# The third weight sum of a seven-product unit: added by a DMA instead of GpSimd, and its product one place later

## The chip, the core and the metric

One core of a Trainium2 chip runs the whole program. The metric is the device time of one execution in microseconds (us); runs of one kernel are compared by their median. The engines are TensorE (PE, matrix products; PEld are its weight loads), VectorE (DVE), ScalarE (ACT), GpSimd (POOL) and SyncE (SP, which here only issues DMAs). Each engine works through its own instruction list in order, and an instruction that waits holds back everything behind it on that engine. DMAs are issued by SP, ACT or POOL and run on sixteen DMA engines.

## What is computed

One step of a two-branch encoder layer over 576 frames (512 of a prompt, 64 of a stream), in float32: a gated feed-forward block, a mixer (a state-space branch, band attention and a matrix memory, merged by gates), and a second feed-forward block.

```python
def swiglu(x, w_in, w_out):
    a, b = jnp.split(x @ w_in, 2, axis=-1)
    return (jax.nn.silu(a) * b) @ w_out

def layer(x, lp, st):
    h = x + 0.5 * swiglu(rmsnorm(x, lp['norm_ffn1']), lp['w_ffn1_in'], lp['w_ffn1_out'])
    mix, new_st = mixer(rmsnorm(h, lp['norm_mix']), lp, st)
    h = h + mix
    h = h + 0.5 * swiglu(rmsnorm(h, lp['norm_ffn2']), lp['w_ffn2_in'], lp['w_ffn2_out'])
    return h, new_st
```

Nearly all the time goes into the products with the weights: `w_ffn1_in` and `w_ffn2_in` (1024 x 8192), their `w_out` (4096 x 1024), and the mixer's `w_in` (1024 x 9752).

## The kernel before

**Units of seven products.** Most of the weight products are done in the manner of Strassen and Winograd: a block of 1024 rows of weights by two column tiles of 128 is taken as four quarters (0 to 3, each 128 partitions x 512), the activations as two halves of the frames (288 each), and eight quarter products become seven. Such a unit needs four sums of weight quarters: X1 = q0 + q1, X2 = q1 + q2, X3 = X1 + q2, X4 = X3 + q3; the products A11, A22 and A21 use quarters 0, 2 and 3 as they are. There are 115 units: 40 in each feed-forward layer (28 that make gated hidden tiles, `swiglu`, and 12 that add to the residual) and 35 in the mixer.

**Splitting.** Each weight operand is split into a high and a low part: ScalarE copies it to a reduced format (tile ph, line 288), VectorE subtracts that from the original (tile pl, line 289). Each product is then 12 matmuls of 128 x 288 on PE (line 616): four row tiles by three combinations of high and low parts.

**Where the sums come from.** `fetch_sums` has SP load quarters 0 and 1 side by side into a tile x12 (ring "wx", four buffers, 128 x 1024), and returns a function that adds quarters 1 and 2 onto it by an adding DMA that GpSimd issues (line 461): x12 then holds X1 and X2. `fetch` has SP load quarters 0, 2 and 3 (ring "wr", five buffers; line 467). `operand` makes X3 and X4 by GpSimd additions (line 472). In the feed-forward layers both are made in place, over X1 and then over X3, so X3's sum waits until X1 has been split, and X4's until X3 has. In the mixer they go to two buffers of the ring "wy", both made when the first of them is asked for.

**Order.** `stream` walks through the units' products in a fixed order (the tuples `order` in `pairs` for the mixer and in `ffn`; a 1 ahead of a product means that it belongs to the unit before). For each product it makes the operand of the product five places on (`AHEAD`), then issues the matmuls, then the read-out of the accumulator. ph and pl have six buffers each, so a split can be six operands ahead of PE. `make` starts the loads of a unit two units ahead, and the adding DMA of the unit after next when X3 is made. From this text a scheduler puts each engine's instructions into their final order, by its own estimate of when each can run.

**Accumulators.** A product adds onto an accumulator that an earlier one began: X3, A22 and X2 onto that of X1, A21 onto that of X4. Between two such products the running sum is read out (by ScalarE: uv, line 533, g, line 627, P, line 632; by VectorE: lines 542, 629, 635, 639, 655), and PE must wait for that read-out. The mixer has three banks for this, the feed-forward layers six. Between the products the mixer's PE also works on the branches' own small matmuls (`tick`, `jobs`).

Of the kernel before, what the change touches and what calls it, by code (L numbers as in the profile page):

```python
# [28 lines left out]
ALU = mybir.AluOpType  # L29
# [52 lines left out]
class Hybrid:  # L82
# [369 lines left out]
    def fetch_sums(self, desc):  # L452


        nc = self.nc
        i = len(self.splan)
        self.splan.append(desc)
        src = self.I["sblk"][i].rearrange("p (q c) -> p q c", q=4)
        x12 = self.ring("wx", shape=(128, 2, 512))
        nc.sync.dma_start(x12, src[:, 0:2, :])  # L460
        return {"x12": x12, "src": src}, lambda: nc.gpsimd.dma_start(x12, src[:, 1:3, :], accum_op=ALU.add)  # L461
# [6 lines left out]

    def operand(self, raw, t):

        x12 = raw["x12"]
        add = lambda o, one, two: self.nc.gpsimd.tensor_tensor(o, one, two, op=ALU.add)  # L472
        if not self.mixer:

            if t in (self.T_X3, self.T_X4):
                add(x12[:, 0, :], x12[:, 0, :], raw[2 if t == self.T_X3 else 3])
            x3 = x4 = x12[:, 0, :]
        else:
            if t in (self.T_X3, self.T_X4) and "x3" not in raw:
                raw["x3"], raw["x4"] = self.ring("wy"), self.ring("wy")  # L480
                add(raw["x3"], x12[:, 0, :], raw[2])
                add(raw["x4"], raw["x3"], raw[3])
            x3, x4 = raw.get("x3"), raw.get("x4")
        return self.parts({self.T_X1: x12[:, 0, :], self.T_X2: x12[:, 1, :], self.T_X3: x3, self.T_X4: x4,
                           self.T_A11: raw[0], self.T_A22: raw[2], self.T_A21: raw[3]}[t])

    def stream(self, seq, order, banks):

# [31 lines left out]
    def pairs(self, seq):  # L520

        nc = self.nc
        order = ((0, self.T_X1), (0, self.T_A11), (1, self.T_A22), (0, self.T_X4), (0, self.T_X3), (1, self.T_X2),
                 (0, self.T_A21))
        H = (slice(0, FH), slice(FH, T))

        def tmp(ps, scale):  # L530
            o = self.gp.tile([128, FH], F32, name="uv", tag="uv", bufs=4)
            with self.tc.high_priority(offset=EVAC):
                nc.scalar.activation(o, ps, AF.Copy, scale=scale)  # L533
            return o

        def emit(ps, scale, other=None, op=None):
            def go(dst, a=0, b=FH, func=None):
                with self.tc.high_priority(offset=EVAC):
                    if other is None:
                        nc.scalar.activation(dst, ps[:, a:b], func or AF.Copy, scale=scale)  # L540
                        return
                    nc.vector.scalar_tensor_tensor(dst, ps[:, a:b], scale, other[:, a:b], op0=ALU.mult, op1=op)
                if func:
                    nc.scalar.activation(dst, dst, func)
            return go

        def pair(tiles, done):
            ((name, c1), s1, put1), ((_, c2), s2, put2) = tiles
            o = {}

            def on(t, ps):
                if t == self.T_X1:
                    o["v"] = tmp(ps, s1)
                elif t == self.T_X4:
                    o["m6"] = tmp(ps, s2)
                elif t == self.T_A11:
                    put1(1, H[1], emit(ps, s1, o["v"], ALU.add))
                elif t == self.T_X3:
                    o["u"] = tmp(ps, s2)
                elif t == self.T_A21:  # L560
                    put2(1, H[1], emit(ps, s2, o["u"], ALU.subtract))
                elif t == self.T_A22:
                    put2(0, H[0], emit(ps, -s2, o["m6"], ALU.add))
                else:
                    put1(0, H[0], emit(ps, s1))
                    if done:
                        done()
            return (name, 0, c1, c2), self.T, on

        self.stream([pair(*p) for p in seq], order, lambda n: {self.T_X1: n % 2, self.T_X4: 2, self.T_A11: 2})  # L570
# [113 lines left out]
    def ffn(self, x, g0, win, wout, name, last=(0, 1)):  # L684
# [3 lines left out]
        nc = self.nc  # L688
# [63 lines left out]
        def unit(c, j):  # L752
            def done(g):
                got[c, j] = g
                flush()
            return (win, 0, 4096 + at(c, j), at(c, j)), self.T, self.swiglu(done)

        def out(c, m):
            def done():
                free[0] = True  # L760
                if c == 2:
                    self.hidden_tiles(name)
                flush()
            return (wout, 1024 * c, 256 * m, 256 * m + 128), self.T2, self.residual(x, m, done if m == 3 else None)
# [4 lines left out]
        seq = [unit(0, j) for j in range(NPLAIN, 8)]  # L769
        for c in range(1, 4):  # L770
            seq += [unit(c, j) for j in range(2)] + [out(c - 1, m) for m in range(4)] + [unit(c, j) for j in range(2, 8)]
        order = ((0, self.T_X1), (1, self.T_A22), (0, self.T_A11), (1, self.T_A21), (0, self.T_X3), (1, self.T_X2),
                 (0, self.T_X4))
        self.stream(seq, order, lambda n: {self.T_X1: n % 3, self.T_A11: 3, self.T_X4: 4 + n % 2})
        self.drain()
# [833 lines left out]
```

## Time and profile before

| | |
|---|---|
| median of 3 runs | 1939.52 us (1937.3 to 1940.52) |
| the profiled execution | 1944.79 us, its span 1943.1 us |
| mean clock that TensorE was granted | 0.991 of full speed |
| first feed-forward layer / mixer's units / second feed-forward layer | about 50 to 600 / 610 to 1205 / 1410 to 1940 us |
| data moved by DMA | 294.69 MB, 152 GB/s on the mean |

The profile is of one execution. Its page gives, for each engine, busy time, share of the span and instruction count; the costliest groups of instructions by line, with the tile written and the tiles read (`wx<-wx,wr`), their count, their busy time, the mean of one in ns, and after the second bar the time in which the engine sat idle just before them and what ended most of it. A list of waits says who waited for whom: total us, how many times, the longest. A table of stretches gives the busy us of each engine in a part of the span, with instruction counts in brackets. The timeline lists instructions with start and duration in us (`x2`: two in a row). Among the DMA rows, an issue has its count, its size and the median us from issue to landing, and q0 is the queue of the DMAs that GpSimd issues (packets, MB, share of the sixteen engines' time).

### The profile page before, as it was taken

The page shows a single profiled execution, that of the slowest core. Times are in us where ns is not written, and L with a number is a line of the kernel's source. Part 1 is how long each engine was busy: PE and PEld are TensorE (multiplying, and loading weights), DVE is VectorE, ACT ScalarE, POOL GpSimd, SP SyncE. Part 2 cuts the span into 40 slices and gives each one's busy share as a digit, 9 for nine tenths or more (in the row PEclk, how much of TensorE's full clock was granted, in tenths as well). Part 3 has the DMA queues.
Part 4 walks back from the last instruction along what each step waited for, and adds up shares of the span by engine and source line. Part 5 has one row for each costly group of instructions (what it writes and reads, how often), then busy time and mean ns, then how long its engine had stood idle before and what let it go on. Part 6 is the DMA issues. An engine that isn't in the chain of part 4 may idle for free. (4 is left out here: it accounts for less than half of the span.)

```text
span 1943.1 us, 37678 instructions
## 1 busy us (share of the span) xinstructions
PE 1887.2 (97%) x13901; PEld 1823.6 (94%) x13901; DVE 1524.6 (78%) x2715; ACT 1089.5 (56%) x2486; POOL 680.1 (35%) x656
## 2 busy tenths in 40 slices
PE   9999999999999999999999998999999999999998
PEld 8899999999999878888888888999999999999998
DVE  8998998988768767667777775745898888988865
ACT  4554654655544777767675765324555455554544
POOL 5343333333202234323435353440233334334311
PEclk9999999999999999899999999999999999999999
DMA  7267666666742545753667557742236666666631
GB/s 241 74 160 173 159 163 163 159 172 163 185 131 80 156 117 159 200 147 108 183 165 183 155 152 213 241 143 88 77 99 165 163 157 172 166 157 167 159 94 60
DMA packets 129440, 294.69 MB, mean 152 GB/s; under 512 B 14289, under 2 KB 26193, under 8 KB 129257
## 3 DMA queue, kind: packets, MB, share of 16 engines
q1 hardware_dynamic: 100072, 205.67, 32.7%
q0 software_dynamic: 19696, 72.10, 20.5%
q10 hardware_dynamic: 9488, 14.53, 2.6%
q8 instruction: 109, 1.79, 0.4%
q14 instruction: 75, 0.61, 0.1%
HBM read 272.87 MB, written 19.38 MB: 150 GB/s over the span
## 5 line engine op out<-in xcount | busy, mean ns | idle before, releaser
L616 PE MATMUL acc<-TH,ph 128*128 128x288 f32 x3220 | 968.0, 301 | 27.4 <-ACT uv L533 11.8
L616 PE MATMUL acc<-TL,ph 128*128 128x288 f32 x3220 | 955.4, 297 | 0.6 <-DVE TL L289 0.6
L616 PE MATMUL acc<-TH,pl 128*128 128x288 f32 x3220 | 955.0, 298 | 1.0 <-DVE pl L289 0.9
L616 PEld LDWEIGHTS acc<-TH,ph 128*128 128x128 f32 x3220 | 607.5, 189 | 46.9 <-ACT uv L533 15.5
L616 PEld LDWEIGHTS acc<-TL,ph 128*128 128x128 f32 x3220 | 609.4, 189 | 4.9 <-issue 3.7
L616 PEld LDWEIGHTS acc<-TH,pl 128*128 128x128 f32 x3220 | 608.4, 189 | 4.8 <-DVE pl L289 2.2
L289 DVE TENSOR_TENSOR pl<-wr,ph 128x512 fp32r<-128x512 f32 x471 | 429.4, 919 | 76.9 <-ACT ph L288 64.5
L288 ACT CAST ph<-wr 128x512 fp32r<-128x512 f32 x471 | 287.9, 620 | 267.9 <-PE acc L616 141.3
L289 DVE TENSOR_TENSOR pl<-wx,ph 128x512 fp32r<-128x512 f32 x390 | 328.1, 845 | 44.5 <-ACT ph L288 37.9
L288 ACT CAST ph<-wx 128x512 fp32r<-128x512 f32 x390 | 237.4, 621 | 201.3 <-POOL wx L472 110.2
L472 POOL TENSOR_TENSOR wx<-wx,wr 128x512 f32<-128x512 f32 x160 | 246.3, 1539 | 188.2 <-DVE pl L289 150.4
L461 POOL DMA_DIRECT2D wx<-in_sblk x115 | 101.6, 901 | 524.1 <-DMA wx<-in_sblk 154.7
L260 PE MATMUL acc<-YH,ph 128*128 128x256 f32 (+1 forms) x768 | 226.5, 298 | 6.3 <-ACT YH L288 5.8
L260 PE MATMUL acc<-YL,ph 128*128 128x320 f32 (+1 forms) x768 | 227.1, 297 | 2.3 <-DVE YL L339 1.9
L260 PE MATMUL acc<-YH,pl 128*128 128x256 f32 (+1 forms) x768 | 226.5, 296 | 0.1
L260 PEld LDWEIGHTS acc<-YH,ph 128*128 128x128 f32 x768 | 145.4, 190 | 6.9 <-ACT YH L288 5.9
L260 PEld LDWEIGHTS acc<-YL,ph 128*128 128x128 f32 x768 | 145.4, 189 | 3.5 <-DVE YL L339 3.3
L260 PEld LDWEIGHTS acc<-YH,pl 128*128 128x128 f32 x768 | 145.2, 189 | 0.3 <-DVE pl L289 0.3
L472 POOL TENSOR_TENSOR wy<-wx,wr 128x512 f32<-128x512 f32 x35 | 56.2, 1605 | 136.0 <-DVE pl L289 120.0
L655 DVE SCALAR_TENSOR_TENSOR R<-acc,R 128x288 f32<-128x288 f32 x168 | 75.7, 450 | 18.6 <-PE acc L616 18.1
L288 ACT CAST TH<-g 128x288 fp32r<-128x288 f32 x120 | 51.6, 434 | 59.8 <-POOL g L641 34.6
L289 DVE TENSOR_TENSOR pl<-wy,ph 128x512 fp32r<-128x512 f32 x70 | 59.8, 857 | 29.6 <-ACT ph L288 26.6
(320 smaller groups left out, 2393.4 us busy)
## 6 DMA issues: line engine op xcount, KB each, us to landing
wr<-in_sblk SPq DMA_DIRECT2D x345, 256.0 KB, 3.6
wx<-in_sblk SPq DMA_DIRECT2D x115, 512.0 KB, 3.8
wx<-in_sblk POOLq DMA_DIRECT2D x115, 512.0 KB, 6.8
wr<-in_wblk SPq DMA_DIRECT2D x126, 256.0 KB, 3.0
R<-scr_rows ACTq DMA_DIRECT2D x12, 576.0 KB, 5.9
gs<-g SPq DMA_DIRECT2D x20, 288.0 KB, 4.5
g<-gs POOLq DMA_DIRECT2D x20, 288.0 KB, 3.9
y<-ys POOLq DMA_DIRECT2D x12, 288.0 KB, 3.8
```

Source lines behind the costliest of these rows:

```text
L260: nc.tensor.matmul(ps[:, :n], wt[:, wsl], xx[:, k0 + k, a:a + n], start=(k == 0 and i == 0), stop=(k == nk - 1 and i == 2))
L288: self.nc.scalar.copy(hi, src)
L289: self.nc.vector.tensor_tensor(lo, src, hi.bitcast(F32), op=ALU.subtract)
L461: return {"x12": x12, "src": src}, lambda: nc.gpsimd.dma_start(x12, src[:, 1:3, :], accum_op=ALU.add)
L472: add = lambda o, one, two: self.nc.gpsimd.tensor_tensor(o, one, two, op=ALU.add)
L616: self.nc.tensor.matmul(ps, wt[:, wsl], xx[:, kk, :], start=(start and kk == 0 and i == 0), stop=(kk == 3 and i == 2), skip_group_check=True)
L655: self.nc.vector.scalar_tensor_tensor(o, ps, scale, o, op0=ALU.mult, op1=ALU.add)
```

## The change

The third sum is no longer made by GpSimd. As soon as X1 has been split, an adding DMA that GpSimd issues adds quarter 2 from HBM onto the X1 half of x12, in place, in the feed-forward layers and in the mixer alike. GpSimd adds only X4: in place in the feed-forward layers, into one buffer of "wy" in the mixer. In both orders X3 moves back one place: behind the earlier unit's X2 in the feed-forward layers, ahead of X4 (which had been first) in the mixer.

```diff
     def operand(self, raw, t):
 
-        x12 = raw["x12"]
-        add = lambda o, one, two: self.nc.gpsimd.tensor_tensor(o, one, two, op=ALU.add)
-        if not self.mixer:
-
-            if t in (self.T_X3, self.T_X4):
-                add(x12[:, 0, :], x12[:, 0, :], raw[2 if t == self.T_X3 else 3])
-            x3 = x4 = x12[:, 0, :]
-        else:
-            if t in (self.T_X3, self.T_X4) and "x3" not in raw:
-                raw["x3"], raw["x4"] = self.ring("wy"), self.ring("wy")
-                add(raw["x3"], x12[:, 0, :], raw[2])
-                add(raw["x4"], raw["x3"], raw[3])
-            x3, x4 = raw.get("x3"), raw.get("x4")
-        return self.parts({self.T_X1: x12[:, 0, :], self.T_X2: x12[:, 1, :], self.T_X3: x3, self.T_X4: x4,
-                           self.T_A11: raw[0], self.T_A22: raw[2], self.T_A21: raw[3]}[t])
+        nc, x12 = self.nc, raw["x12"]
+        x4 = x13 = x12[:, 0, :]
+        if t == self.T_X4:
+            if self.mixer:
+                x4 = self.ring("wy")
+            nc.gpsimd.tensor_tensor(x4, x13, raw[3], op=ALU.add)
+        parts = self.parts({self.T_X1: x13, self.T_X2: x12[:, 1, :], self.T_X3: x13, self.T_X4: x4,
+                            self.T_A11: raw[0], self.T_A22: raw[2], self.T_A21: raw[3]}[t])
+        if t == self.T_X1:
+            nc.gpsimd.dma_start(x13, raw["src"][:, 2, :], accum_op=ALU.add)
+        return parts
...
-        order = ((0, self.T_X1), (0, self.T_A11), (1, self.T_A22), (0, self.T_X4), (0, self.T_X3), (1, self.T_X2),
+        order = ((0, self.T_X1), (0, self.T_A11), (1, self.T_A22), (0, self.T_X3), (0, self.T_X4), (1, self.T_X2),
                  (0, self.T_A21))
...
-        order = ((0, self.T_X1), (1, self.T_A22), (0, self.T_A11), (1, self.T_A21), (0, self.T_X3), (1, self.T_X2),
+        order = ((0, self.T_X1), (1, self.T_A22), (0, self.T_A11), (1, self.T_A21), (1, self.T_X2), (0, self.T_X3),
                  (0, self.T_X4))
```

In the changed file the lines behind `operand` are three lower: the adding DMA of the first sums is on line 462, GpSimd's add on 477, the new adding DMA on 481, the matmuls on 613.

How the built programs differ, first on GpSimd, in the residual units of the first feed-forward layer. The names with numbers are single tiles: wx_3441 (before) and wx_3443 (after) belong to unit 20, wx_3590 to unit 21, wx_3725 to unit 22, wx_3858 to 23, wx_3991 to 24. Before:

```order
L461 DMA wx_3725<-in_sblk 128x1024
L472 TENSOR_TENSOR wx_3441<-wx_3441,wr_3586 128x512
L472 TENSOR_TENSOR wx_3441<-wx_3441,wr_3588 128x512
L461 DMA wx_3858<-in_sblk 128x1024
L472 TENSOR_TENSOR wx_3590<-wx_3590,wr_3721 128x512
L472 TENSOR_TENSOR wx_3590<-wx_3590,wr_3723 128x512
L461 DMA wx_3991<-in_sblk 128x1024
```

After:

```order
L462 DMA wx_3725<-in_sblk 128x1024
L481 DMA wx_3443<-in_sblk 128x512
L477 TENSOR_TENSOR wx_3443<-wx_3443,wr_3588 128x512
L462 DMA wx_3858<-in_sblk 128x1024
L481 DMA wx_3590<-in_sblk 128x512
L477 TENSOR_TENSOR wx_3590<-wx_3590,wr_3723 128x512
L462 DMA wx_3991<-in_sblk 128x1024
```

The new DMA (128 x 512) stands where the add of X3 stood: behind the DMA of the first two sums of the unit after next, and ahead of the add of X4.

Second, ScalarE at the same place, the copies to high parts from A11 of unit 20 to A22 of unit 20. Before they are A11, A21 (unit 19), X3, X2 (unit 19), X4, X1 of unit 21, A22:

```order
L288 CAST ph_3762<-wr_3584 128x512
L288 CAST ph_3779<-wr_3439 128x512
L288 CAST ph_3798<-wx_3441 128x512
L288 CAST ph_3816<-wx_3292 128x512
L288 CAST ph_3835<-wx_3441 128x512
L288 CAST ph_3860<-wx_3590 128x512
L288 CAST ph_3878<-wr_3586 128x512
```

After:

```order
L288 CAST ph_3763<-wr_3584 128x512
L288 CAST ph_3780<-wr_3441 128x512
L288 CAST ph_3797<-wx_3292 128x512
L288 CAST ph_3816<-wx_3443 128x512
L288 CAST ph_3835<-wx_3443 128x512
L288 CAST ph_3860<-wx_3590 128x512
L288 CAST ph_3879<-wr_3586 128x512
```

X2 of unit 19 (tile wx_3292) now stands ahead of X3 of unit 20; X3, X4 and the next unit's X1 follow each other without another operand between.

Third, ScalarE in the mixer, from A22 of unit 61 to A21 of unit 62; uv and P are read-outs of accumulators, the g row is a branch's own work. Before, the two rows that read wy are X4 and X3, the one that reads wx is X2 of unit 61:

```order
L288 CAST ph_12819<-wr_12345 128x512
L540 ACTIVATE P_12559<-acc_12510 128x288
L1152 ACTIVATE g_12860<-P_12559,cst_143 128x579
L288 CAST ph_12841<-wy_12838 128x512
L288 CAST ph_12866<-wy_12837 128x512
L288 CAST ph_12883<-wx_12169 128x512
L533 ACTIVATE uv_12817<-acc_12804 128x288
L533 ACTIVATE uv_12835<-acc_12725 128x288
L533 ACTIVATE uv_12900<-acc_12887 128x288
L288 CAST ph_12902<-wr_12566 128x512
```

After, X3 comes first, from x12 itself (wx_12331), then X4 (wy_12841) and X2 (wx_12150):

```order
L288 CAST ph_12797<-wr_12325 128x512
L530 ACTIVATE uv_12795<-acc_12703 128x288
L537 ACTIVATE P_12538<-acc_12489 128x288
L1149 ACTIVATE g_12836<-P_12538,cst_143 128x579
L530 ACTIVATE uv_12814<-acc_12801 128x288
L288 CAST ph_12817<-wx_12331 128x512
L530 ACTIVATE uv_12877<-acc_12864 128x288
L288 CAST ph_12843<-wy_12841 128x512
L288 CAST ph_12860<-wx_12150 128x512
L288 CAST ph_12879<-wr_12545 128x512
```

One of the three read-outs uv now stands right behind the copy of X3, two ahead of it.

## What was predicted

> **What bounds the kernel now.** I read the page's first part, then the table of stretches, then what TensorE waited for.
>
> ```profile
> PE 1887.2 (97%) x13901; PEld 1823.6 (94%) x13901; DVE 1524.6 (78%) x2715; ACT 1089.5 (56%) x2486; POOL 680.1 (35%) x656
> ```
>
> TensorE (PE) is busy 97% of the span, so everything that a faster helper could return lies in the other 3%, 56 us. Stretches, with busy us of each engine and matmuls in brackets (of 50 to 100, 300 to 350, and the mixer):
>
> ```profile
> core 0: us, PE busy (x) PEld busy (x) DVE busy (x) ACT busy (x) POOL busy (x), PEclk, DMA share, GB/s
> 50.00:100.00 50.00, 46.85 (x325) 45.08 (x325) 48.16 (x88) 28.87 (x64) 17.93 (x12) 0.97 0.27 75
> 300.00:350.00 50.00, 50.00 (x377) 50.00 (x376) 44.48 (x68) 25.77 (x53) 18.18 (x16) 1.00 0.65 165
> 633.00:1205.00 572.00, 546.34 (x3957) 494.36 (x3956) 403.66 (x855) 402.15 (x1098) 220.17 (x224) 0.99 0.60 160
> ```
>
> In the middle of a feed-forward layer PE never stops: 377 matmuls in 50 us are 0.1326 us each, so a product (12) takes 1.59 us and a unit of seven products 11.14 us. That is the **pace** everything else has to keep. The mixer holds most of the idle time (26 us), and the first units (50 to 100) another 3. What PE waited for, longest first:
>
> ```profile
> PE acc L616 <- ACT uv L533: 11.8, 12, 2.9
> PE acc L616 <- DVE g L542: 4.6, 4, 1.6
> PE acc L616 <- ACT g L627: 2.6, 7, 0.6
> PE acc L616 <- DVE P L635: 2.0, 8, 0.3
> PE acc L616 <- DVE pl L289: 0.9, 3, 0.4
> ```
>
> Almost all are accumulators that ScalarE or VectorE had not read out yet; an operand (pl) was late three times. So the third sums do not hold PE now.
>
> **What goes and what comes.** GpSimd's groups and its DMA issues (count, then busy us and mean ns; the last two rows give min/median/max ns):
>
> ```profile
> L472 POOL TENSOR_TENSOR wx<-wx,wr 128x512 f32<-128x512 f32 x160 | 246.3, 1539 | 188.2 <-DVE pl L289 150.4
> L461 POOL DMA_DIRECT2D wx<-in_sblk x115 | 101.6, 901 | 524.1 <-DMA wx<-in_sblk 154.7
> L472 POOL TENSOR_TENSOR wy<-wx,wr x35: 1260/1294/3738, 600.2 to 1171.8; 128x512 f32<-128x512 f32 x35
> L472 POOL TENSOR_TENSOR wy<-wy,wr x35: 1276/1297/1817, 602.6 to 1174.3; 128x512 f32<-128x512 f32 x35
> ```
>
> 80 feed-forward adds of 1.54 us and 35 mixer adds of 1.29 us go: 123 + 45 = 168 us of GpSimd. 115 more issues of 0.90 us come: 104 us. GpSimd is busy 35%, so the 64 us themselves are worth nothing on PE. Two side effects matter more. One unit of the feed-forward layer, row by row in the timeline (start, us, engine):
>
> ```profile
> 335.22 0.88 POOL L461 DMA_DIRECT2D wx<-in_sblk  x1 [5.70 <-DVE TL L289]
> 339.65 0.67 DVE L289 TENSOR_TENSOR pl<-wx,ph 128x512 fp32r<-128x512 f32 x1
> 340.40 1.45 POOL L472 TENSOR_TENSOR wx<-wx,wr 128x512 f32<-128x512 f32 x1 [2.21 <-DVE pl L289]
> 340.75 2.49 DVE L289 TENSOR_TENSOR pl<-wx,ph 128x512 fp32r<-128x512 f32 x2
> 341.88 0.62 ACT L288 CAST ph<-wx 128x512 fp32r<-128x512 f32 x1 [0.87 <-POOL wx L472]
> 342.70 0.62 ACT L288 CAST ph<-wx 128x512 fp32r<-128x512 f32 x1
> 343.52 0.68 DVE L289 TENSOR_TENSOR pl<-wx,ph 128x512 fp32r<-128x512 f32 x1
> ```
>
> First, VectorE: a low part (pl) takes 0.67 us alone, but the two beside the add took 2.49, 1.13 us more than two alone. 115 adds fewer give VectorE up to 115 x 1.13 = 130 us back. Where PE is full that is worth nothing; between 50 and 100, where VectorE is busy 48.16 of 50 us, three adds (units 0 to 2) fall away: between 0 and -3 us, I take **-2**, since PE idles there for VectorE.
>
> Second, the new wait, and this is where I expect the time to go. In the feed-forward layers the four sums of a unit share one buffer. The chain X1 split, sum 3, X3 split, sum 4, X4 split was on three compute engines; now a DMA from HBM stands in the middle of it, and it stands in GpSimd's queue behind the DMA of the first two sums of the unit after next. How long DMAs take (size, median us from issue to landing; the next two are single issues at 168.05 and 428.05; then four issues back to back at 26.89, and queue 0's packets in 26.8 to 44.5, 28 to 29 and 43 to 44):
>
> ```profile
> wx<-in_sblk POOLq DMA_DIRECT2D x115, 512.0 KB, 6.8
> wx<-in_sblk POOLq DMA_DIRECT2D x1, 512.0 KB, 5.8
> wx<-in_sblk POOLq DMA_DIRECT2D x1, 512.0 KB, 7.5
> 26.89 3.76 POOL L461 DMA_DIRECT2D wx<-in_sblk  x4
> q0 software_dynamic: 576, 2.10, 64.5%
> q0 software_dynamic: 7, 0.03, 48.3%
> q0 software_dynamic: 18, 0.02, 10.9%
> ```
>
> An adding DMA of 512 KB lands 6.8 us after its issue (5.8 to 7.5 in these two). The four at the start were 576 packets; the first 7 moved between 28 and 29, the last 18 between 43 and 44, so they took about 14.4 us: 3.6 us each, one after the other. So a 256 KB one that is queued behind a 512 KB one lands about 1.8 us after it (bounds: 1.8 if it goes by bytes, 3.6 if it goes by packets, of which it has as many). Now follow GpSimd's order in the changed kernel from the end of one sum 4 to the end of the next: issue of the first sums (6.8 to landing), the third sum behind it (1.8), X3's high part on ScalarE (0.62), its low part on VectorE (0.67), the add of sum 4 (1.45), and some 0.2 of hops between engines (340.32 to 340.40 and 341.85 to 341.88 above): 6.8 + 1.8 + 0.62 + 0.67 + 1.45 + 0.2 = **11.54 us**. Each step waits for the one before it, so no engine's spare time shortens it, and PE's pace is 11.14. The bounds: 5.8 + 1.8 + 2.94 = 10.5 (hidden, PE never notices) and 7.5 + 3.6 + 2.94 = 14.0. I take 11.54, from the median of 115.
>
> What hides it at first: ScalarE may split six operands ahead (six ph buffers), so X1 can be ready five products less one split, 5 x 1.59 - 1.3 = 6.6 us, before PE wants it. The loop eats 0.40 us of this lead a unit. With 40 units a layer, of which I leave out the first four, that is 72 x 0.40 = 29 us over both layers, less the lead twice, 13: **+16**.
>
> Behind the waiting X3 copy on ScalarE stand X4's, then X1's of the next unit (ScalarE's order), so all of them shift; that is why the lead does not recover. Moving X2 ahead of X3 leaves one product (1.59 us) less between A22's read-out by VectorE (P, L635) and X2; that wait was 2.0 us in 8 places. Bounds -2 (VectorE is freed) and 8 x 1.59 = +13; I take 0, since such waits fall into units in which PE waits for the loop anyway.
>
> In the mixer the loop has no force. The matmuls of the units (L616) in its stretch:
>
> ```profile
> 633.00:1205.00 572.00, 435.48 (x2893) 396.56 (x2892) 0.99 0.60 160
> ```
>
> 2893 / 12 are 241 products, 2.37 us each: a unit takes 16.6 us, and sum 4 goes to a buffer of its own. X3 comes three places after X1, so 7.1 us after it; the DMA lands 5 us (alone: 6.8 - 1.8) to 8.6 us (queued) after its issue. ScalarE then stands up to 1.5 us at X3 with read-outs (uv) behind it, for which PE waits: up to 35 x 1.5 = +52. On the other side the waits of 11.8 and 4.6 us in the list above can go: -16. I take **0**: the middle of 5 and 8.6 is under 7.1. The added bytes (115 x 256 KB = 30 MB, by queue 0's row on the page, 72.10 MB for 20.5%, 8.6% of the sixteen DMA engines) lie under a share of 0.65 in the full stretches; at worst they push the 6.8 toward 7.5, which is in the bounds.
>
> ```profile
> q0 software_dynamic: 19696, 72.10, 20.5%
> ```
>
> Sum: -2 + 16 + 0 = +14 us on the profiled execution's 1944.8 us (span 1943.1), 1959. That execution lies 5.3 us above the median of the three runs, 1939.5, so the forecast is 1939.5 + 14, rounded to **1954**.
>
> **The page's price.** The Trainium skill ("DMA: Bandwidth & Descriptors", section "Anatomy of one DMA — SWDGE (gpsimd) path") fits a DMA from GpSimd as 2.0 us plus its bytes at 436 GB/s; that makes 3.2 us for 512 KB and 2.6 for 256 KB, an estimate from that page. By it the loop would be 3.2 + 0.6 + 2.94 = 6.7 us, far below the pace, and the first rival would hold. The trace disagrees: 6.8 us for the adding 512 KB; that is why the rule gets only a small part of that rival's chance.
>
> **Rivals.**
> - *The DMA lands in time* (faster). The loop stays under 11.14 if the two DMAs together need under 8.2 us; the 5.8 us issue gives 7.6. Then what remains is VectorE's 130 us: the waits for VectorE (4.6 + 2.0 + 0.9) and half of those for uv go, -13 with the start's -2 rounded down to **-11: 1928**. For it: the 5.8 row, and X2, moved ahead of X3, frees its buffer one place (1.59 us) earlier for the load that the first sums wait for. Against: the median. 0.27.
> - *Even.* The loop is between 11.1 and 11.3; what it costs and what VectorE returns cancel: **1940**. 0.15.
> - *Slower, the forecast:* 11.3 to 12.0 us a unit: **1954** (1944 to 1985). 0.42.
> - *A DMA priced by packets:* the third sum costs as long as two (3.6), or traffic lifts the first to 7.5. Loop 12.2 to 13.3; at 12.2, 72 x 1.1 - 13 - 2 = +64: **2003**. For it: as many packets as the big one. Against: nothing measured says 2 KB packets cost what 4 KB ones do. 0.08.
> - *The mixer's read-outs stand behind X3* while the feed-forward loop is hidden: half of the 52, with the start's -2: **1964**. 0.08.
>
> **How the numbers follow.** Slower by over 0.2% (3.9 us, about what a measurement of this kernel can tell from no change): 0.42 + 0.08 + 0.08 = 0.58; within: 0.15; faster: 0.27. The likeliest case alone ranges from 1944 to 1985. For 8 in 10 the range takes in the even case, the mixer rival and most of the faster case, whose centre is 1928: 1927 to 1990; outside stay the packet-priced DMA and the lower part of the faster case.
>
> **What the profile after would show.** The new issue (L481) with 256 KB and its landing: near 6 to 9 us from issue supports the loop, under 5 the first rival. ScalarE's copy ph<-wx waiting for a DMA in the feed-forward layers, and units there over 11.2 us: fewer than 377 matmuls in 300 to 350. The add L477 115 times instead of 230 times; VectorE's busy time some 100 us lower, the mean of pl below 919 ns. Wrong would be: 377 matmuls still in that stretch with a landing over 8 us (the lead or the order hides it), or a mixer that changes by more than 16 us either way.

## The result, and the profile after

The changed kernel takes **2045.1 us** (median of 4 runs, 2033.6 to 2048.6) against 1939.7 us: 1.053 times as long, 95% interval 1.0499 to 1.0562. That is +105 us where the prediction had +14.

The profiled execution lasts 2046.9 us in its span. First the page's part 1, then the table of stretches (columns as before; 50 to 100, 300 to 350, the mixer's units), and under them the mixer's units in the kernel before:

```profile
PE 1921.6 (94%) x13901; PEld 1843.1 (90%) x13901; DVE 1345.4 (66%) x2715; ACT 1067.2 (52%) x2486; POOL 606.5 (30%) x656
50.00:100.00 50.00, 44.97 (x324) 43.25 (x323) 47.17 (x92) 28.96 (x65) 19.23 (x14) 1.00 0.38 95
300.00:350.00 50.00, 47.56 (x351) 46.67 (x350) 33.83 (x68) 21.37 (x43) 13.35 (x14) 1.00 0.71 175
649.00:1300.00 651.00, 581.33 (x4020) 520.18 (x4020) 391.85 (x873) 403.62 (x1105) 203.88 (x235) 0.94 0.61 156
```

```profile
626.00:1209.00 583.00, 557.04 (x4025) 504.08 (x4023) 411.74 (x873) 406.02 (x1105) 224.17 (x231) 0.98 0.59 158
```

Between 300 and 350 us TensorE does 351 matmuls where it did 377. In the mixer it does nearly the same number (4020, 4025) in 651 us instead of 583, and the loss is of two kinds: it stands idle for 651 - 581 = 70 us instead of 26, and is busy 24 us longer, at a granted clock of 0.94 instead of 0.98.

From the first to the last unit product of each part (taken from the timeline), the change costs 25.0 us in the first feed-forward layer (460.9 to 485.9), **68.8 in the mixer** (583.1 to 651.9) and 15.1 in the second layer (455.8 to 470.9). The stretches between them, the start and the end give 5 us back. A profiled execution is one of several and not always a middle one: here it is the slowest of four, e11's the slowest of ten.

What was waited for on the whole (total us, times, longest), then GpSimd's groups and the DMA rows of the page:

```profile
PE acc L613 <- ACT uv L530: 24.1, 16, 6.3
PE acc L613 <- DVE P L632: 22.5, 29, 1.7
ACT ph L288 <- DMA wx<-in_sblk: 323.5, 95, 9.5
```

```profile
L477 POOL TENSOR_TENSOR wx<-wx,wr 128x512 f32<-128x512 f32 x80 | 115.7, 1447 | 449.9 <-DVE pl L289 449.9
L462 POOL DMA_DIRECT2D wx<-in_sblk x115 | 101.9, 904 | 223.3 <-DMA wx<-in_sblk 160.2
L481 POOL DMA_DIRECT2D wx<-in_sblk x115 | 106.4, 925 | 190.8 <-DVE pl L289 181.6
q0 software_dynamic: 36256, 102.25, 28.6%
wx<-in_sblk POOLq DMA_DIRECT2D x115, 512.0 KB, 5.7
wx<-in_sblk POOLq DMA_DIRECT2D x115, 256.0 KB, 6.2
```

ScalarE's copies from x12 have no row of waits for a DMA in the kernel before; now they stand 323.5 us in 95 places, 103.2 of them in the mixer's units. TensorE's two largest waits are for read-outs (uv, P), not for operands. By the engine that ended them, its waits in the mixer grew from 18 to 47 us for ScalarE and from 6 to 19 for VectorE; those for GpSimd and DMAs came to 3 together. Here is one such place in the mixer, rows of GpSimd, ScalarE and TensorE's timelines in order of time (start, us, engine; in brackets the idle time before, and who ended it):

```profile
1009.22 0.89 POOL L462 DMA_DIRECT2D wx<-in_sblk  x1 [6.83 <-DMA wx<-in_sblk]
1009.80 1.22 POOL L481 DMA_DIRECT2D wx<-in_sblk  x1
1019.24 0.62 ACT L288 CAST ph<-wx 128x512 fp32r<-128x512 f32 x1 [6.11 <-DMA wx<-in_sblk]
1020.65 0.39 ACT L530 ACTIVATE uv<-acc 128x288 f32<-128x288 f32 x1
1021.09 0.61 PE L613 MATMUL acc<-TH,ph 128*128 128x288 f32 x1 [4.12 <-ACT uv L530]
```

Read from the top: GpSimd stood 6.83 us at the first sums' DMA of a later unit, whose load had not landed. The third sum's DMA was queued behind it and behind its 512 KB, and landed 9.4 us after its issue. ScalarE stood 6.11 us at X3's copy. The read-out uv stood behind that copy and some small work of a branch, and TensorE 4.12 us behind the read-out.

### The profile page after: what moved, and what is told of

The parts are those of the page before. It is cut to its first block, busy times and chain, and to the rows that moved or that the text cites. A ratio compares the mean times of both kernels' runs of the same rounds, so it can differ in the third digit from the quotient of the medians.

```text
span 2046.9 us, 37697 instructions
## 1 busy us (share of the span) xinstructions
PE 1921.6 (94%) x13901; PEld 1843.1 (90%) x13901; DVE 1345.4 (66%) x2715; ACT 1067.2 (52%) x2486; POOL 606.5 (30%) x656
## 5 line engine op out<-in xcount | busy, mean ns | idle before, releaser
L289 DVE TENSOR_TENSOR pl<-wx,ph 128x512 fp32r<-128x512 f32 x425 | 308.4, 732 | 392.4 <-ACT ph L288 388.3
L288 ACT CAST ph<-wx 128x512 fp32r<-128x512 f32 x425 | 255.6, 618 | 487.0 <-DMA wx<-in_sblk 323.5
L289 DVE TENSOR_TENSOR pl<-wr,ph 128x512 fp32r<-128x512 f32 x471 | 335.8, 716 | 52.9 <-ACT ph L288 46.8
L288 ACT CAST ph<-wr 128x512 fp32r<-128x512 f32 x471 | 281.8, 615 | 161.9 <-PE acc L260 102.3
L477 POOL TENSOR_TENSOR wx<-wx,wr 128x512 f32<-128x512 f32 x80 | 115.7, 1447 | 449.9 <-DVE pl L289 449.9
L260 PE MATMUL acc<-YL,ph 128*128 128x256 f32 (+1 forms) x768 | 228.5, 299 | 2.6 <-DVE YL L339 2.3
L462 POOL DMA_DIRECT2D wx<-in_sblk x115 | 101.9, 904 | 223.3 <-DMA wx<-in_sblk 160.2
L481 POOL DMA_DIRECT2D wx<-in_sblk x115 | 106.4, 925 | 190.8 <-DVE pl L289 181.6
L477 POOL TENSOR_TENSOR wy<-wx,wr 128x512 f32<-128x512 f32 x35 | 45.4, 1298 | 159.4 <-DMA wx<-in_sblk 142.4
```

The lines of the kernel that those rows point to most:

```text
L260: nc.tensor.matmul(ps[:, :n], wt[:, wsl], xx[:, k0 + k, a:a + n], start=(k == 0 and i == 0), stop=(k == nk - 1 and i == 2))
L288: self.nc.scalar.copy(hi, src)
L289: self.nc.vector.tensor_tensor(lo, src, hi.bitcast(F32), op=ALU.subtract)
L477: nc.gpsimd.tensor_tensor(x4, x13, raw[3], op=ALU.add)
L481: nc.gpsimd.dma_start(x13, raw["src"][:, 2, :], accum_op=ALU.add)
```

## The experiments

Sixteen kernels, each measured against the kernel before on the same chip. Parts in us, from the profiled execution, first to last unit product; clock is what TensorE was granted in the mixer's units.

| kernel | time, us | ratio (95%) | layer 1 | mixer (clock) | layer 2 |
|---|---|---|---|---|---|
| before | 1939.7 | | 460.9 | 583.1 (0.98) | 455.8 |
| changed | 2045.1 | 1.053 (1.050 to 1.056) | 485.9 | 651.9 (0.94) | 470.9 |
| e1 mixer only | 2013.2 | 1.035 (1.032 to 1.039) | 462.3 | 653.3 (0.94) | 455.3 |
| e2 layers only | 1975.3 | 1.018 (1.017 to 1.020) | 479.5 | 578.4 (0.99) | 473.1 |
| e3 orders only | 1934.7 | 0.996 (0.995 to 0.998) | 460.3 | 575.0 (0.99) | 451.5 |
| e4 DMA only | 2392.4 | 1.232 (1.230 to 1.234) | 659.3 | 639.0 (0.94) | 647.6 |
| e5 spare target | 1976.7 | 1.019 (1.017 to 1.021) | 460.2 | 609.5 (0.96) | 452.2 |
| e6 third first | 1963.2 | 1.012 (1.010 to 1.013) | 467.3 | 597.9 (0.99) | 455.8 |
| e7 X3 later in the mixer | 2010.9 | 1.037 (1.034 to 1.039) | 482.8 | 614.7 (0.96) | 471.5 |
| e8 half the bytes | 1999.7 | 1.030 (1.027 to 1.032) | 471.7 | 628.9 (0.96) | 459.6 |
| e9 unread, mixer | 1928.9 | 0.995 (0.993 to 0.997) | 460.2 | 572.3 (0.99) | 452.1 |
| e10 e6 and e7 | 1948.4 | 1.004 (1.002 to 1.006) | 464.6 | 592.5 (0.97) | 457.2 |
| e11 e7's order, no DMA | 1936.5 | 0.998 (0.997 to 1.000) | 460.0 | 587.1 (0.97) | 452.9 |
| e12 lead of three, before | 1954.2 | 1.008 (1.006 to 1.010) | 468.2 | 571.9 (0.99) | 461.4 |
| e13 e3, lead of three in the mixer | 1930.2 | 0.995 (0.994 to 0.997) | 462.2 | 567.1 (0.99) | 453.5 |
| e14 changed, lead of three in the mixer | 2051.9 | 1.059 (1.056 to 1.061) | 480.5 | 655.2 (0.94) | 472.7 |
| e15 lead of two, before | 1968.6 | 1.015 (1.013 to 1.017) | 465.0 | 582.0 (0.98) | 463.5 |
| e16 all unread | 2002.7 | 1.032 (1.030 to 1.034) | 496.7 | 568.1 (0.99) | 492.9 |

### Which part, and which half of the change: e1 to e4

Theory A: the third sum, now brought by a DMA, is late, and its wait costs the time. Rival B: the new orders of the products cost it.

e1 and e2 choose the old or the new third sum, and the old or the new order, by the part of the program:

```diff
+    def operand(self, raw, t):
+        return (self.operand_dma if self.mixer else self.operand_sum)(raw, t)
```

e2 has `not self.mixer` there. e3 keeps the changed orders with the old `operand`; e4 keeps the changed `operand` with both old orders.

> The change in the mixer alone; both feed-forward layers as before. In the trace of the changed kernel the mixer's units take 651.5 us instead of 582.8 (+68.7), the feed-forward layers 485.6 and 470.6 instead of 460.6 and 455.5 (+25.0 and +15.1). If the parts cost independently of each other, this kernel takes 1939.7 + 69 = 2005 to 2012 us, with a granted clock in the mixer near 0.94. If the loss in the mixer is inherited from the feed-forward layers (a late start, a lower clock), it takes under 1960.

> The change in the two feed-forward layers alone; the mixer as before. Independent parts: 1939.7 + 40 = 1976 to 1984 us, and the period from one sum 4 to the next stays near 11.8 us. Inherited from the mixer: under 1960 (the first layer comes before the mixer, so it cannot inherit; its +25 should stand in any case).

> The changed order of products in both parts, but the third sum made by GpSimd as before, in place in the feed-forward layers and into a buffer of its own in the mixer. Theory A (the late third sum costs the time, the order is harmless): 1932 to 1948 us. Rival B (the order costs it: one product less between two read-outs of the same accumulator bank, in the mixer between A21 and A11 and in the feed-forward layers between A22 and X2): above 1970 us, with the waits of TensorE for uv in the mixer (24.1 us against 11.8) and for P in the feed-forward layers (22.5 against 2.0) as in the changed kernel.

> The third sum by the adding DMA, with the order of products as before: X4 ahead of X3 in the mixer, X3 ahead of X2 in the feed-forward layers. Theory A: as slow as the changed kernel or slower, 2035 to 2100 us, since the sum is wanted one product (1.6 us in the feed-forward layers, 2.4 in the mixer) earlier. Rival B: under 1975 us.

e1 came to 2013.2 us and e2 to 1975.3, each within 2 us of its range: the two parts cost independently, 72 and 35 us. e3 settles the rival: with the new orders and GpSimd's sums the kernel is 6 us **faster** than before. So the whole loss needs the DMA.

e4 was missed by far: 2392 us where 2035 to 2100 was expected. In its mixer the DMA costs 56 us, much as before; its feed-forward layers take 659 and 648. One period there, from the timelines of SP (the load of the later unit's x12), GpSimd and ScalarE:

```profile
397.29 0.33 SPq L461 DMA_DIRECT2D wx<-in_sblk  x1
401.71 0.87 POOL L462 DMA_DIRECT2D wx<-in_sblk  x1 [5.00 <-DVE R L652]
402.29 1.18 POOL L481 DMA_DIRECT2D wx<-in_sblk  x1
410.70 1.14 ACT L288 CAST ph<-wx 128x512 fp32r<-128x512 f32 x2 [9.36 <-DMA wx<-in_sblk]
```

The first sums' DMA stood 5.00 us at the head of GpSimd's queue and issued 4.4 us after SP had issued the load it adds onto. The profile puts that wait down to VectorE, but to three different instructions in the five periods from 347 to 419 us, while the interval from the load's issue is 4.1 to 4.4 us in all five. In the 22 periods between 150 and 520 us for which the trace has the load's landing, the issue stands 0.02 to 0.03 us behind it; so it is the load. The third sum's DMA came straight behind it, and X3's copy began 8.4 us after that issue. The mean period from one sum 4 to the next was 16.7 us in the first layer. In the changed kernel X2 stands ahead of X3, and the first sums' DMA issued 0.8 us on the mean after sum 4 instead of 5.0. So moving X3 back is what keeps the DMA's price at 40 us and not 390.

### The place in GpSimd's queue, and the bytes: e6 and e8

In the feed-forward layers the mean period from sum 4 to sum 4 was 11.9 us in the first layer (units 5 to 39) and 11.7 in the second, worked out from the timelines. One of them, rows of GpSimd and ScalarE in order of time:

```profile
344.77 1.43 POOL L477 TENSOR_TENSOR wx<-wx,wr 128x512 f32<-128x512 f32 x1 [6.69 <-DVE pl L289]
346.43 0.87 POOL L462 DMA_DIRECT2D wx<-in_sblk  x1 [0.23 <-POOL wx L477]
347.26 1.14 ACT L288 CAST ph<-wx 128x512 fp32r<-128x512 f32 x2
349.87 0.86 POOL L481 DMA_DIRECT2D wx<-in_sblk  x1 [2.56 <-DVE pl L289]
354.73 0.62 ACT L288 CAST ph<-wx 128x512 fp32r<-128x512 f32 x1 [1.94 <-DMA wx<-in_sblk]
356.15 1.29 POOL L477 TENSOR_TENSOR wx<-wx,wr 128x512 f32<-128x512 f32 x1 [4.24 <-DVE pl L289]
```

Sum 4 ends at 346.20. ScalarE copies X4 and the next unit's X1 (347.26), and only when X1's low part is made does the third DMA issue (349.87). X3's copy starts at 354.73, sum 4 ends at 357.44. The mean pieces in the first layer: 2.4 us for the two splits, 0.3 to the issue, 6.3 to X3's copy, 2.8 for X3's split and sum 4. The first sums' DMA, issued in between, is not a step of this loop, but its 512 KB go ahead of the third sum's 256.

e6 orders the two the other way round; e8 adds only half of quarter 2:

```diff
# e6
+                    with (self.tc.issue_after(raw[n]["third"]) if "third" in raw[n] else nullcontext()):
+                        begin.pop(m)()
# e8
-            nc.gpsimd.dma_start(x13, raw["src"][:, 2, :], accum_op=ALU.add)
+            nc.gpsimd.dma_start(x13[:, 0:256], raw["src"][:, 2, 0:256], accum_op=ALU.add)
```

> The changed kernel, with one order fixed: on GpSimd the DMA of the first sums stands behind the third sum's DMA of the unit two earlier, not ahead of it. In the feed-forward layers the period is read as 2.4 (X4 and X1 split) + 0.3 + 6.2 (issue to X3's copy) + 2.8 (X3 split and sum 4) = 11.8 us; without a 512 KB transfer ahead of it the third sum landed in 4.8 us at best, so the period falls to 10.4, under TensorE's pace of 11.14. Theory A: first layer 460 to 466 us (485.9 changed), second 452 to 458 (470.9), mixer 590 to 630 (651.9), the kernel 1950 to 1990. Rival (the path of the forecast: sum 4, then the first sums' DMA, then the third behind it): the period can't fall below 11.1 and the layers stay within 5 us of the changed kernel, the kernel above 2020.

> The changed kernel with only half of quarter 2 added (256 of 512 columns, so 128 KB instead of 256 KB; X3 and X4 leave the other half out). If the landing goes by bytes, it falls by 0.9 us or more (6.2 to about 5.3), the period in the feed-forward layers to 10.9, under the pace: first layer 462 to 470 us, second 453 to 460, the kernel 1985 to 2010. If it goes by packets or by a fixed cost, the landing stays between 5.9 and 6.3 us and the kernel within 10 us of the changed one (2035 to 2055).

The adding DMAs on the pages of e6 (first two rows) and of e8, with queue 0's packets of e8:

```profile
wx<-in_sblk POOLq DMA_DIRECT2D x115, 512.0 KB, 8.3
wx<-in_sblk POOLq DMA_DIRECT2D x115, 256.0 KB, 5.1
```

```profile
wx<-in_sblk POOLq DMA_DIRECT2D x115, 128.0 KB, 5.5
q0 software_dynamic: 36256, 87.18, 25.1%
```

With the third sum ahead, it lands in 5.1 us instead of 6.2, the mean period falls to 11.4 and 11.3 us (nearly TensorE's pace of 11.14), and the kernel to 1963 us: **82 of the 105 us hang on the order of two DMA issues.** The first layer missed its range by 1.3 us here and by 1.7 in e8. Since all 115 DMAs with all their bytes are still there, their traffic can cost the layers little more than what is left: 6 and 0 us against the kernel before, 7 and 4 against e3, which has the same order without the DMA. e8 has as many packets as the changed kernel but half the bytes, and lands 0.7 us sooner, between the two outcomes expected (0.9 or more, 0.3 or less): the price goes by bytes in part, not by packets alone. The Trainium skill ("DMA: Bandwidth & Descriptors", section "Anatomy of one DMA — SWDGE (gpsimd) path") gives 2.6 us for 256 KB, an estimate by its fit; no median of these adding DMAs in any run is under 4.3.

### Waiting or traffic in the mixer: e5, e9 and e16

Rival C: the added traffic and the 115 issues cost the time. e5 sends the mixer's third DMAs onto one spare tile; e9 issues them onto x12 as before, but after X3 and X4 have been made; e16 does that in all units. Nobody reads what they bring, and X3 and X4 leave quarter 2 out there. e5 and e9 have e3's feed-forward layers.

```diff
# e5
+            nc.gpsimd.dma_start(self.spare, raw["src"][:, 2, :], accum_op=ALU.add)
# e9 (in the mixer) and e16 (everywhere)
-        if t == self.T_X1:
+        if t == self.T_X4:
```

> Feed-forward layers as in the kernel with the changed orders and GpSimd's sums (460 and 452 us). In the mixer the new DMA is issued at the same place with the same bytes, but adds onto a spare tile that nobody reads, so X3 and X4 leave quarter 2 out. Theory A (the wait for the landing costs the time, through the read-outs queued behind the waiting copy): the mixer takes 560 to 585 us with a clock of 0.98 or more, the kernel 1918 to 1945 us. Rival C (traffic on the DMA engines and GpSimd's issues cost it): the mixer stays at 630 to 655 us and the clock at 0.94, the kernel at 1990 to 2015 us.

> Feed-forward layers with the changed order and GpSimd's sums. In the mixer all 35 third DMAs are issued with the same bytes onto the same tiles, but after X3 and X4 have been made, so nobody reads what they bring (X3 and X4 leave quarter 2 out) and no spare tile chains them. Theory A (the wait for the landing costs the time): the mixer takes 560 to 585 us, clock 0.98 or more, the kernel 1918 to 1945 us. Rival C (traffic and issues cost it): mixer 630 to 655 us, clock 0.94, the kernel 1990 to 2015.

> The changed kernel, with each third DMA issued when X4 has been split instead of X1, in all 115 units: the same bytes onto the same tiles, but nobody reads what they bring (X3 and X4 leave quarter 2 out). Theory A (the wait costs the time): feed-forward layers of 458 to 463 and 451 to 455 us, a mixer of 567 to 577, the kernel 1918 to 1935. Rival C (30 MB more traffic and 115 more issues cost it): feed-forward layers above 468 and 460 us, the kernel above 1950.

e5 fell between its two ranges (609.5 us) and tells nothing by itself. All its DMAs add onto one tile, so each waits for the one before; eight of them stood in a row on GpSimd at the mixer's start (629 to 665 us), ahead of work that VectorE needed, and TensorE stood still for 27 us. e9 removes that, and the mixer comes to 572.3 us:

```profile
622.00:1194.00 572.00, 549.95 (x4013) 500.09 (x4012) 396.74 (x871) 403.20 (x1104) 196.92 (x227) 0.99 0.69 176
```

The same bytes, at a higher DMA share (0.69 against 0.61), cost the mixer nothing that shows (against e3's 575.0 us it also does one GpSimd sum fewer a unit). **It is the wait.** e16 repeats this in the mixer (568.1), but its feed-forward layers are slower than the changed kernel's: they and the whole time came out in the range given for rival C. There the late DMA holds the shared buffer, and the load of the unit four later must wait for its landing, and the first sums' DMA for that load (SP's and GpSimd's waits):

```profile
SPq L461 <- DMA wx<-in_sblk: 467.5, 75, 11.4
POOL wx L462 <- DMA wx<-in_sblk: 544.9, 85, 11.5
```

So e16 traded one wait for another, as far as these rows show, and can't tell traffic from waiting in the layers. For them the bound on traffic is that of e6.

### Distance and lead in the mixer: e7, e10, e11, e14

e7 puts four products between X1 and X3 in the mixer instead of two; e10 is e6 and e7 together; e11 has e7's order without the DMA; e14 is the changed kernel with operands made three products ahead in the mixer, not five.

```diff
# e7, e10, e11: pairs
-        order = ((0, self.T_X1), (0, self.T_A11), (1, self.T_A22), (0, self.T_X3), (0, self.T_X4), (1, self.T_X2),
-                 (0, self.T_A21))
+        order = ((0, self.T_X1), (1, self.T_A21), (1, self.T_A22), (0, self.T_A11), (1, self.T_X2), (0, self.T_X3),
+                 (0, self.T_X4))
# e14, e13: stream
+        ahead = 3 if self.mixer else AHEAD
```

> The changed kernel, with another order in the mixer: X1, A21 and A22 of the unit before, A11, X2 of the unit before, X3, X4. X3 now follows X1 with four products between instead of two, and three products stand between A11's read-out and X4. Theory A (the third sum is late for ScalarE, which is up to five operands ahead): ScalarE's wait for a DMA at these copies falls from 103 us in the mixer to under 50, and the mixer from 651.9 to 590 to 620 us, the kernel 1985 to 2015. Rival (the read-outs' distances on the banks decide): A21 and A22 now stand closer to the products that begin their banks again, so the mixer stays at 645 us or more, the kernel at 2038 or more.

> The changed kernel with both remedies: the third sum's DMA ahead of the first sums' on GpSimd, and in the mixer the order with four products between X1 and X3. Alone they took the mixer from 651.9 to 597.9 and to 614.7 us. Theory A (each only brings X3's landing and its use closer, and what is left over is small): 575 to 592 us in the mixer, feed-forward layers as with the first remedy alone (467 and 456), the kernel 1938 to 1957 us. If the second remedy costs its own waits (read-outs closer to their banks' next product): 595 us or more, the kernel 1960 or more.

> No third DMA at all: GpSimd's sums, the changed order in the feed-forward layers, and in the mixer the order with four products between X1 and X3. It shows what that order costs or gives by itself. With the other order GpSimd's sums gave a mixer of 575.0 us. If the order is neutral: 570 to 580 us, the kernel 1930 to 1940; if its shorter distances cost waits on the banks: 585 or more, the kernel 1945 or more.

> The changed kernel, with operands made three products ahead instead of five in the mixer. Theory A (X3's landing is late against the interval between X1's split and X3's, three products, which the lead doesn't change): the mixer stays at 635 us or more, the kernel at 2030 or more. Rival D (ScalarE is too far ahead: it stops at X3's copy long before TensorE wants it, with the read-outs behind; nearer to its use the copy waits less): the mixer at 585 to 620 us, the kernel at 1975 to 2015.

Who waited for the third sum's DMA in the changed kernel's mixer (us, times), then ScalarE's wait for it in e7's (us, times, longest):

```profile
  POOL wy L477: 142.4, 32
  ACT ph L288: 103.2, 25
```

```profile
ACT ph L288 <- DMA wx<-in_sblk: 31.2, 6, 11.6
```

With X3 later (e7) ScalarE's wait falls from 103.2 to 31.2 us, as expected, and the mixer to 614.7. The control e11 had 587.1 in the profiled execution (1945 us); its median, 1936.5, is only 2 us above e3's. So what that order costs by itself lies between 2 and 12 us and stays open. With both remedies (e10) ScalarE waits 2.8 us, and the mixer is 592.5 us, half a us past its range and 5 above the control: the DMA's price is then nearly gone. In e14 nothing is gained: 655.2 us. So ScalarE is not too far ahead. What counts is the interval from X1's split to X3's, which a shorter lead leaves as it is.

The waits do not add up to one engine. e6 leaves ScalarE 73.8 us of waiting in the mixer and loses 23 us against e3; e7 leaves 31.2 us and loses 28 against e11. VectorE stands behind ScalarE, and GpSimd waits for the same landing ahead of X4's sum (142.4 us in the changed mixer), each with the branches' work behind it. By what ended TensorE's waits ScalarE's share is the largest (29 of the 44 us of added idle time, VectorE 12), but which of the three queues stood first was not separated.

### The clock, and a faster kernel: e12, e13, e15

e12 and e15 shorten the lead in the kernel before, to make TensorE wait without the DMA; e13 is e3 with the shorter lead in the mixer.

```diff
# e12 (e15: 3, 3 and 2)
-WBUFS = {"wr": 5, "wx": 4, "wy": 2, "ph": 6, "pl": 6}
+WBUFS = {"wr": 5, "wx": 4, "wy": 2, "ph": 4, "pl": 4}
-AHEAD = 5
+AHEAD = 3
```

> The kernel before, with four buffers instead of six for the high and low parts and operands made three products ahead instead of five: no third DMA, no added traffic, only a shorter lead, so that TensorE waits more. It asks what lowers the granted clock. If the clock follows TensorE's idle share, stretches with over 8% idle show a clock of 0.96 or less; if the changed kernel's 0.94 in the mixer came from the added DMA traffic, the clock stays at 0.98 or more here, however long TensorE waits. Slower than before in any case: 1990 to 2300 us.

> The kernel before with three buffers for the high and low parts and operands made two products ahead: no third DMA. It asks what lowers the granted clock. If the clock follows TensorE's idle share, a stretch with over 8% idle has a clock of 0.96 or less, and one with over 15% 0.93 or less; if the changed kernel's 0.94 came from the added DMA traffic, the clock stays at 0.98 or more. Expected 2000 to 2300 us.

> GpSimd's sums with the changed orders (1934.7 us), and in the mixer operands made three products ahead instead of five. The kernel before with a lead of three and four buffers had a mixer of 571.9 us (583.1 with five), and the changed orders alone 575.0. If the two gains add: a mixer of 562 to 568 us, the kernel 1922 to 1929. If they are the same waits removed twice: 571 to 577, the kernel 1931 to 1937.

Both short leads cost far less than expected, and TensorE idled no more than some 4% in any part: neither reaches the idle shares that their expectations name. e9 answers half of the question of the clock: with the traffic but without the waits the clock is 0.99. What the lower clocks go with, roughly, is idle time: 0.94 to 0.96 in mixers in which TensorE idles 9 to 11% (changed, e1, e4, e5, e8, e14), 0.96 to 0.99 in the others at 3 to 7%, 0.90 in e4's feed-forward layers at 21%. Stretches of 25 us: two of the changed kernel's mixer, one of e9, and the one of e5 in which TensorE stood still:

```profile
725.00:750.00 25.00, 25.00 (x146) 18.25 (x144) 14.10 (x36) 17.34 (x49) 6.41 (x10) 0.83 0.35 86
1125.00:1150.00 25.00, 22.55 (x140) 21.52 (x140) 12.84 (x34) 15.44 (x45) 8.15 (x9) 0.80 0.59 160
```

```profile
1100.00:1125.00 25.00, 25.00 (x191) 24.60 (x190) 19.17 (x32) 18.34 (x40) 11.89 (x10) 1.00 0.81 198
```

```profile
650.00:675.00 25.00, 0.00 (x0) 0.00 (x0) 2.14 (x7) 0.48 (x3) 10.83 (x21) 0.55 0.35 56
```

A DMA share of 0.81 goes with a full clock, shares of 0.35 and 0.59 with 0.83 and 0.80; the one full stop has 0.55. The first row shows that a stretch can be wholly busy at a low clock. No run was made for the clock, but the traces' own record of it settles more. It holds full speed and half speed alone, and changes at multiples of 3.41 us. Cut into windows of that length, all eighteen profiled executions together (from 60 us after the start to 60 before the end) show half speed behind 166 of the 166 windows at full speed in which TensorE idled 2.0 us or more, behind 67 of the 203 with 1.2 to 2.0 us, and behind 7 of the 9149 with less. Of the 166, 50 had a DMA share over 0.65 and 116 less. So idle time within a window lowers the clock, and the traffic plays no part that can be seen. The changed mixer was at half speed for 72 us, the one before for 21; at half a us each that makes 26 us, an estimate, near the 24 by which TensorE was busy longer.

The Trainium skill ("TensorE: Matmul & The Clock Gate", section "HAM oscillation — how this bites in real kernels") has it as a rule that a gap of more than some 3.4 us puts the array at half speed. The stop in e5 agrees. But here shorter gaps did it too: of the 240 falls counted, 146 had no gap of 3.4 us in the window ahead.

e13's mixer is in the range for gains that add (567.1), its time 1 us above it. e13 at 1930.2 us, and e3 at 1934.7, are faster than both kernels, by 0.5 and 0.4%: the new orders are worth having with the old sums.

## Why the prediction was wrong

The sign was right, the size was not: +105 us where +14 was said, 2045 us outside a range that ended at 1990. With the mixer's term as it was taken, 0, the time would have fallen inside: e2, which has the change in the layers alone, came to 1975.3.

- **What bounds the kernel: right.** TensorE had 56 us of idle time to win and everything to lose; VectorE gave back 179 us (1524.6 to 1345.4, more than the 130 said), and none of it shows at TensorE. The -2 us at the start did not come: 324 matmuls between 50 and 100 us, 325 before.
- **The feed-forward loop: the right kind of step, mis-sized.** Said 11.54 us a period and +16 us; measured 11.9 and 11.7 and +40. The period came out near by luck: two errors cancelled. The path is not "the first sums' DMA (6.8), then 1.8 more": it goes through X4's and X1's splits (2.4) and then the third DMA's own 6.3 and 6.1. And "the loop eats the lead" was sized at 13 us for both layers, while X4, the product with the least, kept 2.2 us of lead on the median and 1.4 at the least from unit 10 on (its low part's end to the first matmul that reads it): TensorE did not wait for operands but for A22's read-out P behind VectorE's waiting split (22.5 us in 29 places, 2.0 before). That was the wait taken at 0, bounds -2 to +13.
- **The mixer, taken at 0 within -16 to +52: the step that failed.** It measured +69, two thirds of the loss. The prediction compared 7.1 us, from X1's product to X3's, with a landing of 5 to 8.6 us after the issue. The landing was about right:

```profile
DMA to landing us min/median/max: 4.2/7.2/9.6
```

  (The third DMA in the mixer's units.) What was left out stands ahead of the issue: X1's split (0.62 + 0.67 = 1.3 us), and 1.7 us on the mean (0.3 to 6.2, units 42 to 74) in which the issue stood in GpSimd's queue. The first sums' DMA ahead of it waits for its load:

```profile
POOL wx L462 <- DMA wx<-in_sblk: 109.3, 21, 15.6
```

  1.3 + 1.7 + 7.2 = 10.2 us, 3.1 late on the mean against 7.1: 108 us over 35 units, an estimate. ScalarE's measured wait there is 103.2, in 25 places; that the two lie so close is partly luck, since the 7.1 is the pace of the kernel before. The upper bound of 1.5 us a unit was half of this. And the bound priced only waiting: 44 us are TensorE's idle time, within that bound, but 24 more are slower matmuls at the lower clock, for which the prediction had no term.
- **The rivals.** "The mixer's read-outs stand behind X3" named the mechanism, with a chance of 0.08 and a price of 26 us, against 44 of idle time and 24 of slower matmuls. "A DMA priced by packets" fell (e8). "It lands in time" and "even" fell: X3's copy waited for the landing in 95 of the 115 units. The sum of "it lands in time" is also off in itself: -13 and -2 make -15, not -11; nothing else rests on it.
- **What the profile would show.** The landing of 6 to 9 us (6.2), the 351 matmuls, the count of adds and pl's mean (716 ns for pl<-wr, against 919) came as said. A mixer that changes by more than 16 us was named as the sign of an error, and was it.

## What to carry over

When a compute step is replaced by a DMA in the middle of a chain, add up the time from the last use of the old value: the split that frees it, whatever stands ahead of the issue on the issuing engine with that instruction's own wait, the landing with the bytes queued ahead, and only then compare with the distance to the next use. An engine that reaches the new wait in order holds back the read-outs behind it, so the price is paid by an engine that needs none of it. Of two DMAs on one queue, issue the one that is waited for first: here that was worth 82 of 105 us.

## What the runs showed that was not expected

- In the mixer a DMA of the same bytes costs nothing that shows when nobody waits for it: it took 572.3 us with 35 unread ones, 575.0 with none (e9, e3).
- One place in the order of products is worth some 350 us here: DMA with the old orders 2392 us, with the new ones 2045.
- A shorter lead can help: with operands made three products ahead instead of five, and four buffers instead of six, the mixer took 571.9 us instead of 583.1 in the kernel before, while both layers lost 6 to 7 us (e12). Why it helps was not tried.
- TensorE's clock falls to half speed without a long stop: 2 us of idle time within a window of 3.41 us were enough each time, in pieces or in one.
